# A fused decoder layer on one core: activations of the FFN output split beside the FFN's first products

## The chip, the core and the metric

The kernel runs on one core of a Trainium2 chip. The engines are TensorE (PE, with its weight loads as PEld), VectorE (DVE), ScalarE (ACT), GpSimd (POOL) and SyncE (SP), whose queue issues the transfers. The metric is the device time of one execution in microseconds (us).

## The reference, as far as it matters here

One decoder layer: a Mamba-2 mixer and an RG-LRU mixer side by side, then a SwiGLU feed-forward network (FFN) on 1024 positions of width 1024, hidden width 2816, all in float32. The change touches the FFN alone:

```python
hn = rmsnorm(h, norm2_w[l])
gate, up = jnp.split(hn @ w_ffn_in[l], 2, axis=-1)
h = h + (jax.nn.silu(gate) * up) @ w_ffn_out[l]
```

## The kernel before, in words

Data lie transposed: a tile has 128 features on the partitions and 1024 positions in two halves of 512. The hidden width is 22 such tiles (NFF), act_d[0] to act_d[21], kept in DRAM. A float32 product is done as three matmuls on operands that are split in two parts of reduced precision: hi is a cast (ScalarE, L98), lo is the value less hi (VectorE, L99), both in split. So one step of 128 by 128 by 512 is the three matmuls of product, L906 to L908.

Large products are done by a scheme of seven products in place of eight, on 2 by 2 blocks, with sums of operand blocks formed ahead. The activation operands of the seven are four blocks (b11, b21, b22 and b12, which is in the sums alone) and four sums t1 to t4; three of the blocks and the four sums are used.

**FFN, first products.** pair(n, ...) makes hidden tile n: gate and up weights, by the activations x2, which are split once and stay in the pool ar (20 of its 22 units) and in ar0. The seven products of a pair, in order, are a11·b11, s1·t1, s2·t2, a12·b21, s3·t3, s4·b22 and a22·t4, 12 matmuls each. The first, third, fifth and seventh go to one PSUM bank pu, which ScalarE copies after the first (L1250) and third (L1256), and which VectorE adds after the fifth (L1265) and reads after the seventh (L1272). In between the weights of the next pair are made: casts and subtractions (pair_a1, pair_s1, pair_s) and four sums on GpSimd (pair_sums, L1136 to L1139). finish_pair multiplies by the norm (L1204, L1206), takes the Silu (L1205), multiplies gate by up (L1207) and stores act_d[n]. After each product pump() puts a piece of other work into the program; ScalarE's instructions of a pair are pinned in the order in which they are written.

**t_store.** For the FFN output the sums t1 to t4 of the activations are made beforehand: eight calls of t_store in pairs 6 to 9 and 14 to 17, as work of pump(). Each loads two tiles of act_d, does four subtractions of half width (L301, L302, L304, L305) and stores two tiles t_d. In the order as built their instructions stand up to a pair earlier, so that pair 17 has none.

**FFN output.** seven(...) does 8 of the 22 hidden tiles by the scheme; it is called twice (NPART). A slot is half of one of the seven products: 24 matmuls. The second call's slots follow those of the first. Per product, load_xop loads four operand blocks of 128 by 512 (as two units xr of 512 KB) four slots ahead, x_part splits them two slots ahead, w_part splits weights and products runs. Its results are added to eight tiles res of the residual, which load_res loads. GpSimd forms the weight sums (w_sum, L960, L963). The slots before the first product are run beside the last pair (lead). The remaining six hidden tiles follow as plain products, then the last norm.

A pool's unit is a buffer of 128 by 1024 float32. Instructions of an engine run in the order in which the scheduler has put them; a buffer is used again when its last reader is done.

Of the kernel before, what the change touches and what calls it, by code (L numbers as in the profile page):

```python
# [8 lines left out]
F32 = mybir.dt.float32  # L9
F32R = mybir.dt.float32r  # L10
# [57 lines left out]
def hybrid_block(ctx, tc, xT, w_in, w_dt, w_os, w_ol, w_o, w_fi, w_fo, w_fl, lru_w, params, heads, out):  # L68
# [10 lines left out]
    def store(dst, src):  # L79
        nc.sync.dma_start(out=dst, in_=src)  # L80
# [200 lines left out]
    res_d = [dram.tile([P, T], F32, name=f"res_d{i}") for i in range(KD)]  # L281
    ty_d = [dram.tile([P, T], F32, name=f"ty_d{i}") for i in range(16)]
    tl_d = [dram.tile([P, T], F32, name=f"tl_d{i}") for i in range(8)]
    t_d = [dram.tile([P, T], F32, name=f"t_d{i}") for i in range(8 * NPART)]
    act_d = [dram.tile([P, T], F32, name=f"act_d{i}") for i in range(NFF)]

    def row(t_):
# [2 lines left out]
    def t_store(pool, src, dst, k, swap=False):  # L290


        u1, u2 = unit(pool, F32, "tu"), unit(pool, F32, "tu")
        for u, i in ((u1, k), (u2, k + 4)):
            if swap:
                for h in range(2):
                    load(u[:, h], src[i][:, hcol[1 - h]])
            else:
                load(row(u), src[i])
        yield  # L300
        V.tensor_tensor(u1[:, 0], u1[:, 1], u1[:, 0], op=ALU.subtract)  # L301
        V.tensor_tensor(u1[:, 1], u2[:, 1], u1[:, 1], op=ALU.subtract)  # L302
        yield
        V.tensor_tensor(u2[:, 1], u2[:, 1], u1[:, 0], op=ALU.subtract)  # L304
        V.tensor_tensor(u2[:, 0], u2[:, 0], u2[:, 1], op=ALU.subtract)  # L305
        store(dst[k], row(u1))
        store(dst[k + 4], row(u2))
        yield


# [609 lines left out]
        for f, a in events.pop(slot, ()):  # L920
            f(*a)

    def seven(c0_, act, tdf, w_of, out, pools=None, xpool=None, swap=False, done=None):


        pools = pools or {}
        wr, wop, xr_, xop, banks = {}, {}, {}, {}, {}

        def load_w(q, kh, g):

            if (q, kh) == (0, 0):
                t_ = wpool.tile([P, KD, P], F32, name="raw", tag="raw", bufs=2)
                t_ = t_.rearrange("p (a k) c -> p a k c", a=2)
            else:
                t_ = unit(pools.get((q, kh), ar), F32, "wr").rearrange("p a (k c) -> p a k c", c=P)
            for a in range(2):
                load(t_[:, a], w_of(q * 4 + 2 * g + a, kh))
            wr[q, kh, g] = t_

        def load_xop(n, kk):  # L940

            u = unit(xpool if xpool and n == N1 else ar, F32, "xr")
            src, o, h = {
                N2: (act, 4, 0), N5: (tdf, 0, 0), N3: (act, 4, 1), N1: (act, 0, 0),
                N6: (tdf, 4, 1), N7: (tdf, 0, 1), N4: (tdf, 4, 0),
            }[n]
            if swap and src is act:
                h = 1 - h
            for a in range(2):
                load(u[:, a], src[o + 2 * kk + a][:, hcol[h]])  # L950
            xr_[n, kk] = u

        def x_part(n, kk):
            hi, lo = (unit(xpool if xpool and n == N1 else ar, name=x) for x in ("xph", "xpl"))
            split(row(hi), row(lo), row(xr_.pop((n, kk))))
            xop.setdefault(n, []).extend((hi[:, a], lo[:, a]) for a in range(2))

        def w_sum(n, g):
            w = lambda q, kh: wr[q, kh, g]
            sub = lambda o, a, b: G.tensor_tensor(o, a, b, op=ALU.subtract)  # L960
            if n == 1:
                wr["s1", g] = unit(pools.get("s1", ar), F32, "ws").rearrange("p a (k c) -> p a k c", c=P)
                G.tensor_tensor(wr["s1", g], w(1, 0), w(1, 1), op=ALU.add)  # L963
            elif n == 2:
                sub(w(1, 0), w(0, 0), w(1, 0))
                sub(w(0, 0), wr["s1", g], w(0, 0))
            else:
                sub(w(0, 1), w(0, 1), w(0, 0))

        def w_part(n, g):  # L970
            key = {N2: (0, 1), N5: ("s1",), N3: (0, 1), N1: (0, 0), N6: (0, 0), N7: (1, 0), N4: (1, 1)}[n]
            hi, lo = (wpool.tile([P, 2, 4, P], F32R, name=x, tag=x) for x in ("whi", "wlo"))
            split(hi, lo, wr[(*key, g)])
            wop[n, g] = hi, lo

        def products(n, g):
            first, last = n in (N1, N2, N5), n in (N2, N3, N4)
            q, h = {N2: (0, 0), N5: (1, 1), N3: (0, 1), N1: (0, 0), N6: (0, 1), N7: (1, 1), N4: (1, 0)}[n]
            hi, lo = wop.pop((n, g))
            for a in range(2):  # L980
                p = 2 * g + a
                b = "x" if n == N2 else "v" if n in (N5, N3) else "u", p
                if first:
                    banks[b] = bank()
                product(banks[b], (hi[:, a], lo[:, a]), xop[n], first, last)
                d = q * 4 + p
                r, new = out(d, 1 - h if swap else h)
                if new and n in (N1, N5, N3, N4):
                    S.copy(r, banks[b])
                else:  # L990
                    V.tensor_tensor(r, r, banks[b], op=ALU.add)  # L991
                if done:
                    done(n, d)

        for g in range(2):
            at(c0_ - 4 + g, load_w, 0, 0, g)
            at(c0_ - 3 + g, load_w, 0, 1, g)
            at(c0_ - 2 + g, load_w, 1, 0, g)
            at(c0_ - 2 + g, load_w, 1, 1, g)
            for n in range(7):  # L1000
                at(c0_ + 2 * n - 4 + g, load_xop, n, g)
                at(c0_ + 2 * n - 2 + g, x_part, n, g)
                at(c0_ + 2 * n + g - 1, w_part, n, g)
                at(c0_ + 2 * n + g, products, n, g)
            for n in range(1, 4):
                at(c0_ + n + g, w_sum, n, g)
        rank = {f: r for r, f in enumerate((load_w, load_xop, w_part, x_part, w_sum, products))}
        for s in events:
            events[s].sort(key=lambda e: rank.get(e[0], 0 if e[0] not in later else 9))
# [274 lines left out]
    for i in range(NPART):  # L1284
        seven(
            i * CYC,
            act_d[8 * i : 8 * i + 8],
            t_d[8 * i : 8 * i + 8],
            lambda d, kh, i=i: w_fo[d, :, i * 8 + kh * 4 : i * 8 + kh * 4 + 4],
            lambda d, h: (res[d][:, h, :], False),  # L1290
            pools={"s1": wq, **({(1, 0): ar0} if i == 0 else {k: ar0 for k in ((0, 1), (1, 0), (1, 1))})},
        )
    for d in range(KD):
# [2 lines left out]


    todo = []

    def pump():  # L1300

# [11 lines left out]

    first_pair()
    for j in range(1, NFF):
        k = j - 6
        if 0 <= k < 8 * NPART and k % 8 < 4:
            todo.append(t_store(ar, act_d, t_d, k))
        if j == NFF - 1:
            todo.append(lead())  # L1320
        pair(j, None if j == NFF - 1 else j + 1, pump)
# [167 lines left out]
```

## Time and profile before

| | |
|---|---|
| median of 3 runs | 2103.59 us (2103.03 to 2105.32) |
| the profiled execution's own time | 2101.82 us |
| its span, first to last instruction | 2100.1 us |
| mean granted TensorE clock | 0.983 of full |
| TensorE busy | 2036.4 us, 97% |
| VectorE busy | 1395.7 us, 66% |
| ScalarE busy | 934.6 us, 45% |
| GpSimd busy | 538.0 us, 26% |

Times within the span are counted from its start. The pairs of the FFN's first products run from about 1440 to 1855, the two calls of seven from 1855 to 2020, the plain products and the last norm until 2100. Each engine has its own in-order queue; "idle before" names what ended an engine's wait. A busy share is a mean over stages, so the stage's own rows have to be read.

### The profile page before, as it was taken

What the parts mean: (1) busy time and instruction counts of PE and PEld (TensorE: products, weight loads), DVE (VectorE), ACT (ScalarE), POOL (GpSimd) and SP (SyncE); (2) the same over time, 40 slices, a digit from 0 to 9 for tenths busy, and PEclk for the clock granted to TensorE, in tenths of its full rate; (3) what the DMA queues carried; (4) which work ended last, traced back from release to release, by engine and by line L of the source; (5) the groups of instructions that cost most, each with busy time, mean ns of one, the idle gap of its engine ahead of it and who ended that gap; (6) DMA issues with size and microseconds to landing.
All of it is one profiled execution on the core that took longest, in us unless ns stands there. A gap on an engine that the chain in (4) does not pass through costs nothing. (4 is left out here: it accounts for less than half of the span.)

```text
span 2100.1 us, 24937 instructions
## 1 busy us (share of the span) xinstructions
PE 2036.4 (97%) x9506; PEld 1648.4 (78%) x9506; DVE 1395.7 (66%) x1618; ACT 934.6 (45%) x1291; POOL 538.0 (26%) x430
## 2 busy tenths in 40 slices
PE   8999999999999999999989999998999999989998
PEld 5677887887887888888868877776888888868888
DVE  8655567568667548666577868786466466578745
ACT  5334445445445436666643333453333333334334
POOL 5103333234333410000044042332322332242100
PEclk8999999999999999999989999999999999999999
DMA  4222223323223248244464613542254154276112
GB/s 141 86 64 87 89 76 118 100 67 121 93 76 115 89 160 316 95 157 157 154 205 160 231 55 118 165 154 82 74 181 157 66 179 171 86 281 209 61 59 88
DMA packets 121767, 269.85 MB, mean 128 GB/s; under 512 B 13616, under 2 KB 33072, under 8 KB 121648
## 3 DMA queue, kind: packets, MB, share of 16 engines
q1 hardware_dynamic: 121360, 267.22, 37.9%
q8 instruction: 74, 1.21, 0.2%
q10 hardware_dynamic: 288, 1.05, 0.1%
q14 instruction: 45, 0.37, 0.1%
HBM read 205.04 MB, written 63.18 MB: 128 GB/s over the span
## 5 line engine op out<-in xcount | busy, mean ns | idle before, releaser
L174 PE MATMUL pj<-hnh,whi 128*128 128x512 f32 x1152 | 461.3, 400 | 0.0
L176 PE MATMUL pj<-hnl,whi 128*128 128x512 f32 x1152 | 453.2, 393 | 0.0
L175 PE MATMUL pj<-hnh,wlo 128*128 128x512 f32 x1152 | 452.2, 393 | 0.0
L99 DVE TENSOR_TENSOR wlo<-raw,whi 128x1024 fp32r<-128x1024 f32 (+1 forms) x138 | 188.4, 1366 | 186.5 <-ACT whi L98 186.3
L176 PEld LDWEIGHTS pj<-hnl,whi 128*128 128x128 f32 x1152 | 216.8, 188 | 47.6 <-issue 0.5
L174 PEld LDWEIGHTS pj<-hnh,whi 128*128 128x128 f32 x1152 | 217.0, 188 | 45.7 <-issue 2.4
L175 PEld LDWEIGHTS pj<-hnh,wlo 128*128 128x128 f32 x1152 | 217.2, 189 | 44.8 <-issue 1.4
L906 PE MATMUL pbk<-xph,whi 128*128 128x512 f32 x560 | 222.5, 398 | 10.4 <-ACT xph L98 10.3
L908 PE MATMUL pbk<-xpl,whi 128*128 128x512 f32 x560 | 222.1, 398 | 10.1 <-DVE xpl L99 10.1
L907 PE MATMUL pbk<-xph,wlo 128*128 128x512 f32 x560 | 221.9, 396 | 3.2 <-DVE wlo L99 3.2
L98 ACT CAST whi<-raw 128x1024 fp32r<-128x1024 f32 (+1 forms) x138 | 142.5, 1033 | 79.8 <-PE pbk L908 29.4
L963 POOL TENSOR_TENSOR ws<-wr 128x1024 f32<-128x1024 f32 x10 | 29.2, 2920 | 454.1 <-DMA gate_d<-gl 297.0
L908 PEld LDWEIGHTS pbk<-xpl,whi 128*128 128x128 f32 x560 | 107.1, 191 | 36.3 <-DVE xpl L99 14.4
L906 PEld LDWEIGHTS pbk<-xph,whi 128*128 128x128 f32 x560 | 107.2, 191 | 35.3 <-ACT xph L98 13.2
L645 ACT ACTIVATE E<-csb,cs 128x128 f32<-128x128 f32 x256 | 82.8, 391 | 107.6 <-PE yb L686 100.4
L907 PEld LDWEIGHTS pbk<-xph,wlo 128*128 128x128 f32 x560 | 107.2, 191 | 28.1 <-DVE wlo L99 5.9
L99 DVE TENSOR_TENSOR xpl<-xr,xph 128x1024 fp32r<-128x1024 f32 x70 | 108.3, 1555 | 15.4 <-ACT xph L98 12.8
L906 PE MATMUL pbk<-xth,wsh 128*128 128x512 f32 x264 | 107.1, 406 | 4.8 <-DVE c L1228 4.6
L98 ACT CAST xph<-xr 128x1024 fp32r<-128x1024 f32 x70 | 72.9, 1050 | 81.4 <-DVE xpl L99 35.3
L907 PE MATMUL pbk<-xth,wsl 128*128 128x512 f32 x264 | 106.0, 401 | 0.0
L908 PE MATMUL pbk<-xtl,wsh 128*128 128x512 f32 x264 | 106.0, 401 | 0.0
L98 ACT CAST wsh<-raw 128x1024 fp32r<-128x1024 f32 x44 | 46.1, 1050 | 117.2 <-POOL raw L1139 92.4
(303 smaller groups left out, 4110.1 us busy)
## 6 DMA issues: line engine op xcount, KB each, us to landing
raw<-in_w_in SPq DMA_DIRECT2D x74, 512.0 KB, 3.5
raw<-in_w_fi SPq DMA_DIRECT2D x44, 512.0 KB, 3.7
csb<-cs_d SPq DMA_DIRECT2D x64, 256.0 KB, 3.6
act_d<-c SPq DMA_DIRECT2D x22, 512.0 KB, 3.9
yn_d<-xs SPq DMA_DIRECT2D x16, 512.0 KB, 3.4
tu<-yn_d SPq DMA_DIRECT2D x16, 512.0 KB, 6.2
ty_d<-tu SPq DMA_DIRECT2D x16, 512.0 KB, 4.2
xr<-ty_d SPq DMA_DIRECT2D x32, 256.0 KB, 3.4
```

The source lines that it names most:

```text
L98: ins = S.copy(hi, src)
L99: V.tensor_tensor(lo, src, hi.bitcast(F32), op=ALU.subtract)
L174: PE.matmul(ps, wh, xh, start=i == 0, stop=False)
L175: PE.matmul(ps, wl, xh, start=False, stop=False)
L176: PE.matmul(ps, wh, xl, start=False, stop=i == n - 1)
L645: S.activation(E[:, j, :], csb[:, j, :], AF.Relu, bias=cs[:, c, h0 + j : h0 + j + 1], scale=-1.0)
L906: PE.matmul(ps, wh, xh, start=first and k == 0, stop=False, skip_group_check=True)
L907: PE.matmul(ps, wl, xh, start=False, stop=False, skip_group_check=True)
L908: PE.matmul(ps, wh, xl, start=False, stop=last and k == n - 1, skip_group_check=True)
L963: G.tensor_tensor(wr["s1", g], w(1, 0), w(1, 1), op=ALU.add)
```

## The change

t_store of the FFN output and its tiles t_d go. In their place x_split, in every second pair from 6 to 20, loads two tiles of act_d, splits them as they are (the blocks b21, b22 and b11), forms the four sums, splits these too, and stores hi and lo of each of the seven operands side by side in a tile xs_d of DRAM: 14 stores of 256 KB each. hi and lo come from the pool br, which has six units and holds c0 and c1 of the pairs. In the FFN output load_xop loads a finished operand, hi and lo in one unit xp, three slots ahead in place of four, and x_part is not called. Uses in the earlier layers of the kernel keep x_part and t_store. Lines from L284 on are moved down: L1250 is now L1293, L1253 is L1296, L1256 is L1299, L1261 is L1304, L1265 is L1308, L1268 is L1311, L1272 is L1315, L1204 to L1207 are L1247 to L1250, L1136 to L1139 are L1179 to L1182.

```diff
-    t_d = [dram.tile([P, T], F32, name=f"t_d{i}") for i in range(8 * NPART)]
+    xs_d = [
+        [[dram.tile([P, 2, H], F32, name=f"xs_d{i}{n}{b}") for b in range(4)] for n in range(7)] for i in range(NPART)
+    ]
...
+    NX = ("b11", "b21", "t1", "b22", "t2", "t3", "t4")
+
+    def x_split(upool, pool, src, dst, k):
+        u1, u2 = unit(upool, F32, "tu"), unit(upool, F32, "tu")
+        load(row(u1), src[k])
+        load(row(u2), src[k + 4])
+        yield
+
+        def put(u, names):
+            hi, lo = unit(pool, name="xsh"), unit(pool, name="xsl")
+            split(row(hi), row(lo), row(u))
+            for a, n in enumerate(names):
+                if n:
+                    d = dst[NX.index(n)][k % 4]
+                    store(d[:, 0], hi[:, a].bitcast(F32))
+                    store(d[:, 1], lo[:, a].bitcast(F32))
+
+        put(u2, ("b21", "b22"))
+        yield
+        put(u1, ("b11", None))
+        yield
+        V.tensor_tensor(u1[:, 0], u1[:, 1], u1[:, 0], op=ALU.subtract)
+        V.tensor_tensor(u1[:, 1], u2[:, 1], u1[:, 1], op=ALU.subtract)
+        yield
+        V.tensor_tensor(u2[:, 1], u2[:, 1], u1[:, 0], op=ALU.subtract)
+        V.tensor_tensor(u2[:, 0], u2[:, 0], u2[:, 1], op=ALU.subtract)
+        yield
+        put(u1, ("t1", "t3"))
+        yield
+        put(u2, ("t4", "t2"))
         yield
...
         def load_xop(n, kk):
+            if pre:
+                for a in range(2):
+                    u = unit(xpool if xpool and n == N1 else ar, F32, "xp")
+                    load(row(u), pre[n][2 * kk + a].rearrange("p a b -> p (a b)"))
+                    xop.setdefault(n, []).append((u[:, 0].bitcast(F32R), u[:, 1].bitcast(F32R)))
+                return
...
-                at(c0_ + 2 * n - 4 + g, load_xop, n, g)
-                at(c0_ + 2 * n - 2 + g, x_part, n, g)
+                at(c0_ + 2 * n - (3 if pre else 4) + g, load_xop, n, g)
+                if not pre:
+                    at(c0_ + 2 * n - 2 + g, x_part, n, g)
...
     for i in range(NPART):
         seven(
             i * CYC,
-            act_d[8 * i : 8 * i + 8],
-            t_d[8 * i : 8 * i + 8],
+            None,
+            None,
...
+            pre=xs_d[i],
...
+    XSPLIT = (6, 8, 10, 12, 14, 16, 18, 20)
...
     for j in range(1, NFF):
-        k = j - 6
-        if 0 <= k < 8 * NPART and k % 8 < 4:
-            todo.append(t_store(ar, act_d, t_d, k))
+        if j in XSPLIT:
+            i = XSPLIT.index(j)
+            todo.append(x_split(ar, br, act_d[8 * (i // 4) :], xs_d[i // 4], i % 4))
```

How the instructions stand, at three places.

VectorE in pair 16, which had a t_store and now has an x_split. tu are the loaded tiles, wlo, ws1l and wsl the low parts of weights, c the pair's results, xsl the low parts of operands. Before:

```order
L301 TENSOR_TENSOR tu<-tu 128x512
L99 TENSOR_TENSOR wlo<-raw,whi 128x1024
L99 TENSOR_TENSOR ws1l<-ws_13384,ws1h 128x512
L1261 TENSOR_TENSOR c_13310<-c_13310,pbk 128x512
L302 TENSOR_TENSOR tu<-tu 128x512
L304 TENSOR_TENSOR tu<-tu 128x512
L305 TENSOR_TENSOR tu<-tu 128x512
L1265 TENSOR_TENSOR c_13311<-c_13311,pbk 128x512
L1206 TENSOR_TENSOR c_13311<-c_13311,rs_10486 128x512
L99 TENSOR_TENSOR wsl<-raw,wsh 128x1024
L1268 TENSOR_TENSOR c_13310<-c_13310,pbk 128x512
L1204 TENSOR_TENSOR c_13310<-c_13310,rs_10486 128x1024
```

Now, from the first split of the pair to its last instruction, in two pieces:

```order
L99 TENSOR_TENSOR xsl<-tu,xsh 128x1024 x2
L335 TENSOR_TENSOR tu<-tu 128x512
L99 TENSOR_TENSOR wlo<-raw,whi 128x1024
L1304 TENSOR_TENSOR c_13480<-c_13480,pbk 128x512
L336 TENSOR_TENSOR tu<-tu 128x512
L99 TENSOR_TENSOR ws1l<-ws_13562,ws1h 128x512
L338 TENSOR_TENSOR tu<-tu 128x512
L1308 TENSOR_TENSOR c_13481<-c_13481,pbk 128x512
L339 TENSOR_TENSOR tu<-tu 128x512
L99 TENSOR_TENSOR xsl<-tu,xsh 128x1024
L1249 TENSOR_TENSOR c_13481<-c_13481,rs_10526 128x512
```

```order
L1311 TENSOR_TENSOR c_13480<-c_13480,pbk 128x512
L99 TENSOR_TENSOR wsl<-raw,wsh 128x1024
L99 TENSOR_TENSOR xsl<-tu,xsh 128x1024
L1315 TENSOR_TENSOR c_13481<-pbk,rs_10526 128x512
L99 TENSOR_TENSOR wsl<-raw,wsh 128x1024
L1247 TENSOR_TENSOR c_13480<-c_13480,rs_10526 128x1024
L1250 TENSOR_TENSOR c_13480<-c_13480,c_13481 128x1024
```

Four full-width subtractions xsl have come in, and the subtractions of the sums stand between the weights' and the results' instructions.

ScalarE in the same pair, from the copy of the first product to that of the next pair. xsh are the high parts of operands, whi, ws1h and wsh those of weights. Before:

```order
L1250 COPY c_13310<-pbk 128x512
L1253 COPY c_13311<-pbk 128x512
L1256 COPY c_13310<-pbk 128x512
L98 CAST whi<-raw 128x1024
L98 CAST ws1h<-ws_13384 128x512
L98 CAST wsh<-raw 128x1024 x2
L1205 ACTIVATE c_13310<-c_13310 128x1024
L1250 COPY c_13446<-pbk 128x512
```

Now:

```order
L1293 COPY c_13480<-pbk 128x512
L1296 COPY c_13481<-pbk 128x512
L98 CAST xsh<-tu 128x1024 x2
L1299 COPY c_13480<-pbk 128x512
L98 CAST whi<-raw 128x1024
L98 CAST ws1h<-ws_13562 128x512
L98 CAST wsh<-raw 128x1024
L98 CAST xsh<-tu 128x1024 x2
L98 CAST wsh<-raw 128x1024
L1248 ACTIVATE c_13480<-c_13480 128x1024
L1293 COPY c_13644<-pbk 128x512
```

Two casts xsh stand ahead of the third product's copy, and two between the weights' casts; the Silu and the next pair's first copy follow as before.

SyncE's transfers ahead of the FFN output, in and behind the last pair (act_d_230, act_d_270 are hidden tile 20; act_d_231, act_d_271 tile 21; wr are weights, res the residual, xr and xp operands). Before, from the residual tiles on:

```order
L77 DMA res_14048<-res_d_165 128x1024
L77 DMA res_14050<-res_d_164 128x1024
L77 DMA res_14052<-res_d_163 128x1024
L77 DMA res_14054<-res_d_162 128x1024
L77 DMA xr<-act_d_212 128x512
L77 DMA xr<-act_d_213 128x512
L77 DMA wr<-in_w_fo 128x512 x4
L77 DMA xr<-act_d_214 128x512
L77 DMA xr<-act_d_215 128x512
L77 DMA wr<-in_w_fo 128x512 x4
L77 DMA xr<-act_d_216 128x512
L77 DMA xr<-act_d_217 128x512
```

The rows that followed were the store of act_d_231 and the other four res. Now, from the load of the second operand tile (xs_d_195) to the last of the second product (xs_d_201), in two pieces:

```order
L77 DMA xp<-xs_d_195 128x1024
L77 DMA wr<-in_w_fo 128x512 x4
L77 DMA xp<-xs_d_196 128x1024
L77 DMA xp<-xs_d_197 128x1024
L77 DMA res_14307<-res_d_165 128x1024
L77 DMA res_14309<-res_d_164 128x1024
L77 DMA res_14311<-res_d_163 128x1024
L77 DMA res_14313<-res_d_162 128x1024
L77 DMA wr<-in_w_fo 128x512 x4
L77 DMA xp<-xs_d_198 128x1024
L77 DMA xp<-xs_d_199 128x1024
```

```order
L80 DMA act_d_271<-c_14224 128x1024
L77 DMA res_14373<-res_d_169 128x1024
L77 DMA res_14375<-res_d_168 128x1024
L77 DMA res_14377<-res_d_167 128x1024
L77 DMA res_14379<-res_d_166 128x1024
L77 DMA xp<-xs_d_200 128x1024
L77 DMA xp<-xs_d_201 128x1024
```

The first four res have moved behind operands and weights, and all eight stand ahead of the last two tiles of the second product.

## Rows read from the trace of the kernel before

**Rows 1.** The page, first part: busy us (share of span) and instructions, TensorE.

```profile
PE 2036.4 (97%) x9506; PEld 1648.4 (78%) x9506; DVE 1395.7 (66%) x1618; ACT 934.6 (45%) x1291; POOL 538.0 (26%) x430
```

**Rows 2.** Who waited, 1440 to 1856: engine, line, releaser, us, times, longest.

```profile
PEld pbk L906 <- DVE c L1265: 2.8, 8, 0.7
```

**Rows 3.** Timeline, ScalarE, pairs 16 to 18: start, us, engine, line, [idle before].

```profile
1741.63 0.59 ACT L1250 COPY c<-pbk 128x512 f32<-128x512 f32 x1 [1.07 <-PE pbk L908]
...
1759.02 1.06 ACT L1205 ACTIVATE c<-c 128x1024 f32<-128x1024 f32 x1 [2.44 <-DVE c L1204]
...
1761.17 0.59 ACT L1250 COPY c<-pbk 128x512 f32<-128x512 f32 x1 [1.08 <-PE pbk L908]
...
1763.89 0.59 ACT L1253 COPY c<-pbk 128x512 f32<-128x512 f32 x1 [2.13 <-DMA raw<-in_w_fi]
...
1780.58 0.59 ACT L1250 COPY c<-pbk 128x512 f32<-128x512 f32 x1 [1.53 <-PE pbk L908]
```

**Rows 4.** Timeline, TensorE, the FFN output: first matmul, one wait, last matmul.

```profile
1855.29 0.39 PE L906 MATMUL pbk<-xph,whi 128*128 128x512 f32 x1
...
1857.73 0.50 PE L908 MATMUL pbk<-xpl,whi 128*128 128x512 f32 x1 [1.59 <-DVE xpl L99]
...
2019.59 0.39 PE L908 MATMUL pbk<-xpl,whi 128*128 128x512 f32 x1
```

**Rows 5.** Who TensorE waited for, 1855 to 2000.

```profile
PE pbk L908 <- DVE xpl L99: 4.1, 3, 2.1
PE pbk L906 <- ACT xph L98: 2.1, 1, 2.1
PE pbk L907 <- DVE wlo L99: 1.0, 2, 0.8
```

**Rows 6.** Stretches: length, PE, PEld, DVE, ACT, POOL busy, clock, DMA, GB/s.

```profile
1847.00:1875.00 28.00, 22.51 (x92) 16.79 (x90) 20.86 (x17) 10.99 (x11) 17.49 (x7) 0.93 0.95 344
1855.00:1860.00 5.00, 3.41 (x15) 2.48 (x15) 4.90 (x5) 1.99 (x2) 0.55 (x2) 1.00 0.93 333
1872.00:1876.00 4.00, 1.70 (x4) 0.98 (x4) 4.00 (x3) 2.56 (x3) 4.00 (x2) 0.50 1.05 392
1876.00:1880.00 4.00, 3.62 (x9) 2.33 (x9) 4.00 (x2) 0.00 (x0) 4.00 (x2) 0.50 0.45 166
```

**Rows 7.** Timeline, VectorE, the FFN output's early splits of activations.

```profile
1872.06 10.02 DVE L99 TENSOR_TENSOR xpl<-xr,xph 128x1024 fp32r<-128x1024 f32 x3
```

**Rows 8.** Timeline, VectorE, full-width instructions back to back.

```profile
1837.85 1.22 DVE L1207 TENSOR_TENSOR c<-c,c 128x1024 f32<-128x1024 f32 x1
1838.99 1.22 DVE L99 TENSOR_TENSOR wlo<-raw,whi 128x1024 fp32r<-128x1024 f32 x1
```

**Rows 9.** Timeline, VectorE, in pair 16, which has a t_store.

```profile
1750.46 0.68 DVE L1261 TENSOR_TENSOR c<-c,pbk 128x512 f32<-128x512 f32 x1
1751.06 1.19 DVE L302 TENSOR_TENSOR tu<-tu 128x512 f32<-128x512 f32 x1
1752.28 1.67 DVE L304 TENSOR_TENSOR tu<-tu 128x512 f32<-128x512 f32 x1
1753.98 0.69 DVE L305 TENSOR_TENSOR tu<-tu 128x512 f32<-128x512 f32 x1
1754.59 0.68 DVE L1265 TENSOR_TENSOR c<-c,pbk 128x512 f32<-128x512 f32 x1
```

**Rows 10.** Timeline, GpSimd's weight sums in pair 16.

```profile
1745.35 1.29 POOL L1136 TENSOR_TENSOR ws<-raw 128x512 f32<-128x512 f32 x1 [11.48 <-DMA raw<-in_w_fi]
...
1750.09 1.61 POOL L1138 TENSOR_TENSOR raw<-ws,raw 128x512 f32<-128x512 f32 x1 [2.07 <-DVE wlo L99]
...
1751.78 1.62 POOL L1139 TENSOR_TENSOR raw<-raw 128x512 f32<-128x512 f32 x1
```

**Rows 11.** Timeline, SyncE's DMA issues, pair 21: start, us of issuing.

```profile
1839.46 5.98 SPq L77 DMA_DIRECT2D res<-res_d  x4
...
1847.55 0.80 SPq L77 DMA_DIRECT2D xr<-act_d  x2
```

More of the change, by code (lines that the diff above doesn't have):

```diff
@@ L307, in t_store @@
         store(dst[k + 4], row(u2))
+        yield
[24 more added lines that the diff above has]
+        put(u1, ("t1", "t3"))
+        yield
+        put(u2, ("t4", "t2"))
         yield
@@ L921, in run, with seven @@
             f(*a)
-    def seven(c0_, act, tdf, w_of, out, pools=None, xpool=None, swap=False, done=None):
+    def seven(c0_, act, tdf, w_of, out, pools=None, xpool=None, swap=False, done=None, pre=None):
         pools = pools or {}
```

## The prediction

> **What bounds the kernel now.** Read the page's first part first: TensorE is busy 97% of the span [rows 1]. A change can then gain only where TensorE stands, and loses wherever it makes TensorE stand. So the next view is who TensorE waits for in the two stages that the change touches.
>
> In the FFN's first products (pairs 1 to 21) it waits for almost nothing. One row [rows 2] is the one to learn from: eight times a weight load waited for VectorE's L1265, 2.8 us together and 0.7 at most. Eight is the number of t_store calls here. Already the four half-width subtractions of a t_store bring VectorE to the edge of a pair. L1265 adds the fifth product's bank and so frees it for the seventh product.
>
> ScalarE's rows [rows 3] give the beat. L1250 copies the first product's bank, 1761.17 and 1780.58 in the next pair: 19.41 us without a t_store. The pair before, with one, took 1761.17 - 1741.63 = 19.54. From L1250 to L1253, 2.72 us, is one product of 12 matmuls, 0.227 us each.
>
> In the FFN output the first and the last matmul stand 164.3 us apart [rows 4]; 672 matmuls of 0.227 are 152.3, so 12.2 us are lost (with the last matmul's own 0.2). The waits that the trace names make 4.1 + 2.1 + 1.0 = 7.2 of them [rows 5], all behind splits on ScalarE and VectorE; the other 5.0 are small gaps and the clock, which stood at 0.50 of full, 1.2 GHz, from 1872 to 1880 [rows 6]. Behind the longest stretch is one row [rows 7]: three splits that take 1.14 us elsewhere [rows 8] needed 10.02, beside GpSimd's weight sums. These 12.2 us are all that the change can win back there.
>
> **What goes from the FFN output.** 28 splits of activations per engine, 1.14 us each on VectorE, leave this stage. The three slow ones with them, so I take the waits on operand splits as gone. That is the gain: at most 12.2 us, if nothing else comes late.
>
> **What comes into the pairs.** Eight x_splits in pairs 6, 8, ... 20, each wholly inside one pair. Each has the four half-width subtractions of a t_store, plus four full-width splits (one cast on ScalarE and one subtraction on VectorE each), plus 14 stores of 256 KB for two of 512.
>
> I time such a pair by the order of its VectorE instructions, with time 0 at its L1250 copy (L1293 now). The second copy ends 2.72 + 0.59 = 3.31 later. The first cast of an x_split stands behind it and takes 1.05 as the other casts, so VectorE's first split starts at 4.36. From there to the multiplication by the norm (L1247, formerly L1204), the order has 18 instructions: eight of full width, 1.14 us from start to start [rows 8], and ten of half width, 0.60 [rows 9]. That is 9.12 + 6.00 = 15.12 us without a gap.
>
> Then waits on GpSimd. The half-width subtraction that takes 0.60 took 1.22 and 1.70 from start to start beside GpSimd's second pair of sums, while additions that read a PSUM bank, at 1750.46, went by in 0.60 [rows 9]. Each finished just after a sum did [rows 10]: a VectorE instruction with both inputs in SBUF stands while a sum runs. This costs 0.62 + 1.10 = 1.72 us, as it does now. The first two sums, 1.29 us each, begin 3.72 after the copy, one behind the other [rows 3, 10], where VectorE idles now. There the first two new splits will stand. The trace has no such meeting in a pair; the bounds are 0 and 2 x 1.29 = 2.58. I take 0.65 for what is left of the first sum at 4.36 and 1.29 for the second, 1.94, since the splits of the output stage waited for whole sums [rows 7].
>
> L1247 thus ends at 4.36 + 15.12 + 1.72 + 1.94 = 23.14. The Silu behind it on ScalarE takes 1.06 [rows 3] and ends at 24.20. ScalarE is in order: the next pair's L1293 copy stands behind this Silu, and ends at 24.79. The third product of the next pair adds into the bank that this copy reads, and would start at 19.41 + 2.72 = 22.13. So it is **2.66 us late**. (About 1.3 of that falls already before the seventh product: L1308, behind eight instructions of 6.42 us and the same waits, ends at 4.36 + 6.42 + 3.66 + 0.60 = 15.04, and six products end at 5 x 2.75 = 13.8.) The pair after has no x_split and VectorE catches up, so nothing adds up beyond this.
>
> Eight times 2.66 is 21.3 us; the eight t_stores' own 0.13 each, 1.0 in all, go: **+20.3 us**. With no waits for the first two sums it would be 8 x 0.72 - 1 = +4.8, with the full 2.58 it would be 8 x 3.30 - 1 = +25.4. The casts, 4.2 us of ScalarE per pair, cost nothing beyond this: the first two fill its 2.13 us of idling ahead of a copy [rows 3], the other two wait for VectorE. The transfers of such a pair (14 stores, two operand loads, two weight loads and one store of activations, 6.3 MB in 19.4 us or 325 GB/s) stay below the 344 seen over 28 us [rows 6]; if this cover went, the weights, GpSimd's sums and with them L1308 would come later still.
>
> **The transfers ahead of the FFN output.** The operands now come as two parts, 2 MB for each of the seven products where 1 MB came. They need units of the pool ar, which holds the operands of the last pair until its fifth product. Now the first load that needs one is issued at 1847.55, 7.74 us before the output's first matmul [rows 4, 11]. In the new order of the queue, a load of the second operand tile stands at that point, and the residual tiles that went out at 1839.46, while the units were still held [rows 11], have moved behind it. From there to the last tile of the second product (xs_d_201) I count seven operand tiles, eight residual tiles, four half-MB pieces of weights and one store, 20 pieces of 0.524 MB or 10.5 MB, where 14 loads of 0.262 stood before the corresponding tile. At 344 GB/s [rows 6] this takes 30.5 us and ends 22.8 after the output's first matmul. The second product needs that tile after 48 + 9 matmuls, 12.9 us. **9.9 us late.** The nearest other rate, 392 GB/s over 4 us [rows 6], makes it 6.2.
>
> The Trainium skill (DMA: Bandwidth & Descriptors, Where 436 GB/s comes from) gives about 358 GB/s as one core's share of HBM; by that it would be 8.7 late and my sum 1.2 us shorter. The 392 of the trace lies above this figure, so it is no hard limit here.
>
> After such a wait I expect the clock at 1.2 GHz again, as from 1872 on, and leave the 5.0 us of clock and small gaps as they are: 9.9 + 5.0 = 14.9 us lost in place of 12.2, **+2.7**. At 392 GB/s it is 6.2 + 5.0, or -1.0; with twice the clock loss of now (5.3 us of matmuls ran at half speed from 1872 to 1880 [rows 6], 2.7 lost) and as much again for transfers that start late, it is +8.
>
> **Sum.** The profiled execution took 2101.82 us, 1.77 below the median of the runs. 2101.8 + 20.3 + 2.7 = 2124.8 on that basis; as a median, 2126.6. Forecast **2127 us**. What a measurement can tell from no change is 0.2%, 4 us.
>
> **The rivals.**
> 1. The operands land in time. For it: the queue runs ahead and some units may free earlier. Against: 10.5 MB in 20 us would be 510 GB/s, which no stretch shows. Were it so, the output stage would lose some 3 us for 12.2: 2127 - 12 = 2115.
> 2. Faster, the other side: the pairs hide the splits. The point that decides is VectorE's margin: 22.13 - 0.59 - 1.06 - 15.12 - 4.36 = 1.0 us of waiting per pair. Against: 1.72 are waited already by the rows of now. With it hidden, -1 us in the pairs, and -9 in the output if its operands come in time too: 2103.6 - 10 = 2094.
> 3. No difference: pairs hide the splits (-1) and the output's transfers take back its gain (+2.7): 2105.
> 4. The clock falls in the pairs. A fall at the output cost 2.7 us above; with five falls among the sixteen waits it is 2127 + 13 = 2140. Against: from 1855 to 1860, with a wait of 1.59 us in it [rows 4], the clock stayed at 1.00 [rows 6], and my waits are no longer and over 5 us apart.
>
> **How the numbers follow.** The forecast's own case 0.57, its range 2107 to 2137 by the bounds above (+4.8 - 1.0 and +25.4 + 8, and 1.8 to the median). Rival 1, 0.18; rival 2, 0.08; rival 3, 0.08; rival 4, 0.09. The range 2103 to 2138 leaves out rival 2 and most of rival 4. Faster 0.09, the same 0.08, slower 0.83.
>
> **What would show it.** Right: TensorE rows that wait on VectorE's L1308 and on ScalarE's L1293, about eight of each and over 1 us; full-width xsl splits of over 2 us beside GpSimd's L1179 and L1180; pairs of 20.7 and 20.8 us where an x_split sits or has just sat; in the output's first 25 us one wait of several us that ends with a transfer of xs_d, and a clock of 0.50 behind it; no split waits there. Wrong: pairs of 19.4 us throughout, with L1247 ending before 21 us after its copy; or an output stage of less than 157 us.

## The result, and the profile after

The changed kernel takes 2115.69 us (median of 4 runs, 2114.18 to 2117.61), the kernel before, on the same chip, 2103.31 (2102.39 to 2105.32). The ratio is 1.0057, 95% interval 1.0045 to 1.007: slower by 12.4 us, where 23 were forecast. The profiled execution took 2115.78 us with a span of 2114.1, 14.0 more than before. The profiled execution before had been 1.5 below its own median, which is the difference between 14.0 and 12.4. All of the following sums are made on the spans.

The page's first part, to be held against [rows 1] (busy us, share of the span, instructions):

```profile
PE 2037.0 (96%) x9506; PEld 1645.6 (78%) x9506; DVE 1403.2 (66%) x1622; ACT 935.3 (44%) x1295; POOL 537.8 (25%) x430
```

TensorE does the same work and is busy for the same time; its share fell because it stands longer. So the first view is again whom it waits for, in the FFN's first products (engine, line, releaser: us in all, times, longest):

```profile
PE pbk L942 <- ACT c L1293: 8.9, 8, 1.1
PE pbk L942 <- DVE c L1308: 6.0, 8, 0.8
PE pbk L942 <- DVE c L1271: 4.5, 1, 4.5
```

The third row is the first pair's and was there before the change. The first two are new, eight times each, once for every x_split. In TensorE's timeline of pairs 16 and 17 they are these:

```profile
1767.48 0.50 PE L942 MATMUL pbk<-xth,wsh 128*128 128x512 f32 x1 [0.73 <-DVE c L1308]
...
1777.12 0.50 PE L942 MATMUL pbk<-xth,wsh 128*128 128x512 f32 x1 [1.11 <-ACT c L1293]
```

ScalarE's timeline shows how they fall into the beat (start, us, engine, line, idle before), for the answer to [rows 3]:

```profile
1752.97 0.59 ACT L1293 COPY c<-pbk 128x512 f32<-128x512 f32 x1 [1.58 <-PE pbk L944]
...
1775.53 1.06 ACT L1248 ACTIVATE c<-c 128x1024 f32<-128x1024 f32 x1 [5.43 <-DVE c L1247]
1776.50 0.57 ACT L1293 COPY c<-pbk 128x512 f32<-128x512 f32 x1
...
1794.15 0.59 ACT L1293 COPY c<-pbk 128x512 f32<-128x512 f32 x1 [1.57 <-PE pbk L944]
```

Pair 16 takes 23.53 us and pair 17 takes 17.65. The short pair does not mean a fast TensorE: its first copy came late, because ScalarE stood 5.43 us for VectorE's L1247 and then did the Silu. Two pairs take 41.18 where 38.82 is the beat of before, 2.36 us for each x_split.

VectorE in the same pair, answering to [rows 9]:

```profile
1757.21 3.47 DVE L99 TENSOR_TENSOR xsl<-tu,xsh 128x1024 fp32r<-128x1024 f32 x2 [4.05 <-ACT xsh L98]
...
1762.46 0.68 DVE L1304 TENSOR_TENSOR c<-c,pbk 128x512 f32<-128x512 f32 x1
1763.05 1.47 DVE L336 TENSOR_TENSOR tu<-tu 128x512 f32<-128x512 f32 x1
1764.45 1.78 DVE L99 TENSOR_TENSOR ws1l<-ws,ws1h 128x512 fp32r<-128x512 f32 x1
...
1766.75 0.68 DVE L1308 TENSOR_TENSOR c<-c,pbk 128x512 f32<-128x512 f32 x1
...
1774.29 1.21 DVE L1247 TENSOR_TENSOR c<-c,rs 128x1024 f32<-128x1024 f32 x1
```

And GpSimd's sums, answering to [rows 10]:

```profile
1756.01 1.29 POOL L1179 TENSOR_TENSOR ws<-raw 128x512 f32<-128x512 f32 x1 [11.03 <-DMA raw<-in_w_fi]
1757.38 2.22 POOL L1180 TENSOR_TENSOR raw<-raw 128x512 f32<-128x512 f32 x1
1762.68 1.30 POOL L1181 TENSOR_TENSOR raw<-ws,raw 128x512 f32<-128x512 f32 x1 [3.09 <-DVE wlo L99]
1764.06 1.62 POOL L1182 TENSOR_TENSOR raw<-raw 128x512 f32<-128x512 f32 x1
```

The two xsl splits have the first two sums beside them, of L1179 only its last 0.1 us; L336 and ws1l have the other two. L1304, which reads a PSUM bank and runs while L1181 starts, takes its plain 0.68. The sum loses time too: L1180 took 2.22 us beside the splits and 1.30 in pair 17, which has none.

In the FFN output TensorE's timeline answers to [rows 4] and its named waits to [rows 5]:

```profile
1873.66 0.39 PE L942 MATMUL pbk<-xp,whi 128*128 128x512 f32 x1
...
1885.70 0.47 PE L942 MATMUL pbk<-xp,whi 128*128 128x512 f32 x1 [0.46 <-DMA xp<-xs_d]
...
1894.49 0.50 PE L942 MATMUL pbk<-xp,whi 128*128 128x512 f32 x1 [2.31 <-DMA xp<-xs_d]
...
1895.77 0.80 PE L942 MATMUL pbk<-xp,whi 128*128 128x512 f32 x1 [0.22 <-DMA xp<-xs_d]
...
2033.45 0.39 PE L944 MATMUL pbk<-xp,whi 128*128 128x512 f32 x1
```

```profile
PE pbk L942 <- DMA xp<-xs_d: 3.0, 3, 2.3
PE pbk L943 <- DVE wlo L99: 1.1, 2, 0.7
```

The stage takes 159.8 us where it took 164.3. The waits on splits of activations are gone; three short ones on transfers have come. The stretches around the longest (length, busy PE, PEld, DVE, ACT, POOL, clock, DMA share, GB/s) answer to [rows 6]:

```profile
1895.00:1897.00 2.00, 1.78 (x5) 1.06 (x5) 0.00 (x0) 0.00 (x0) 2.00 (x1) 0.55 1.02 412
...
1875.00:1903.00 28.00, 23.90 (x92) 17.61 (x91) 10.72 (x12) 4.85 (x5) 17.44 (x7) 0.94 1.03 407
```

Behind the wait of 2.31 the clock stood near 1.2 GHz (0.55 of full in the first of the two stretches) for some 3 us, and the transfers ran at 407 GB/s over 28 us.

The account of the 14.0 us: the pairs, from the second pair's first copy (1449.92, before 1449.16) to the output's first matmul, took 423.7 us for 406.1, **+17.6**; the output **-4.5**; what lies ahead of the pairs +0.8 and behind the output +0.1.

### The profile page after: what moved, and what is told of

It reads as the page before. It is cut to its first block, busy times and chain, and to the rows that moved or that the text cites. A ratio compares the mean times of both kernels' runs of the same rounds, so it can differ in the third digit from the quotient of the medians.

```text
span 2114.1 us, 25171 instructions
## 1 busy us (share of the span) xinstructions
PE 2037.0 (96%) x9506; PEld 1645.6 (78%) x9506; DVE 1403.2 (66%) x1622; ACT 935.3 (44%) x1295; POOL 537.8 (25%) x430
## 3 DMA queue, kind: packets, MB, share of 16 engines
q8 instruction: 74, 1.21, 0.2%
## 5 line engine op out<-in xcount | busy, mean ns | idle before, releaser
L942 PE MATMUL pbk<-xph,whi 128*128 128x512 f32 x336 | 134.0, 399 | 8.8 <-ACT xph L98 8.8
L944 PE MATMUL pbk<-xpl,whi 128*128 128x512 f32 x336 | 134.3, 400 | 5.3 <-DVE xpl L99 5.3
L943 PE MATMUL pbk<-xph,wlo 128*128 128x512 f32 x336 | 133.6, 398 | 2.9 <-DVE wlo L99 2.9
L942 PE MATMUL pbk<-xth,wsh 128*128 128x512 f32 x264 | 107.2, 406 | 19.5 <-ACT c L1293 8.9
L1033 DVE TENSOR_TENSOR res<-res,pbk 128x512 f32<-128x512 f32 x96 | 65.1, 683 | 73.5 <-PE pbk L944 73.3
L943 PE MATMUL pbk<-xth,wsl 128*128 128x512 f32 x264 | 105.1, 398 | 0.0
L1179 POOL TENSOR_TENSOR ws<-raw 128x512 f32<-128x512 f32 x22 | 29.0, 1319 | 252.7 <-DMA raw<-in_w_fi 241.7
L942 PE MATMUL pbk<-xp,whi 128*128 128x512 f32 x224 | 88.3, 394 | 3.0 <-DMA xp<-xs_d 3.0
L943 PE MATMUL pbk<-xp,wlo 128*128 128x512 f32 x224 | 88.0, 393 | 1.1 <-DVE wlo L99 1.1
L944 PE MATMUL pbk<-xp,whi 128*128 128x512 f32 x224 | 87.5, 392 | 0.0
```

The lines of the kernel that those rows point to most:

```text
L942: PE.matmul(ps, wh, xh, start=first and k == 0, stop=False, skip_group_check=True)
L943: PE.matmul(ps, wl, xh, start=False, stop=False, skip_group_check=True)
L944: PE.matmul(ps, wh, xl, start=False, stop=last and k == n - 1, skip_group_check=True)
L1179: G.tensor_tensor(blk(s1), u_[:, 0:4, :], u_[:, 4:8, :], op=ALU.add)
```

## The experiments

Theory: in a pair with an x_split VectorE's in-order chain is too long, counted in its own instructions and in the time it stands beside GpSimd's sums. Rivals: the new transfers, or ScalarE's new casts. For the output: the order of the transfer queue. In each run "pairs" is the time from the second pair's first copy to the output's first matmul (changed kernel 423.7), "output" that from its first to its last matmul (159.8). The runs fell on several chips, on which the kernel before took 2101.5 to 2103.3 us; so whole times are compared by their ratio to it, and stages by the traces.

**No low parts.** In put of x_split:

```diff
-            hi, lo = unit(pool, name="xsh"), unit(pool, name="xsl")
-            split(row(hi), row(lo), row(u))
+            hi = unit(pool, name="xsh")
+            S.copy(row(hi), row(u))
...
-                    store(d[:, 1], lo[:, a].bitcast(F32))
+                    store(d[:, 1], hi[:, a].bitcast(F32))
```

> Edit: in x_split the low part is not subtracted; the high part is stored in its place, so the casts, the stores and the loads stay and eight times four full-width VectorE subtractions go (the FFN output is computed with a wrong low part). Theory: an x_split's pair is late because VectorE's chain is too long, and without 4 x 1.14 = 4.56 us of it L1247 ends about 4.6 earlier, well before the 22.13 that the third product needs. All pairs then take 19.4 to 19.6 us in place of 23.5 and 17.7 in turn, and the time falls by 8 x 2.36 = 18.9, to 2096 to 2099 us. Rival one, transfers: the 14 stores of an x_split delay weights and so the pair. Then pairs stay at 23.5 and 17.7 and the time at 2113 to 2117. Rival two, ScalarE's four casts: the same, no gain.

Measured: 2091.88 us, ratio to before 0.9952 (0.9933 to 0.997). The first copies of pairs 16 to 18:

```profile
1739.97 0.59 ACT L1293 COPY c<-pbk 128x512 f32<-128x512 f32 x1 [1.53 <-PE pbk L944]
...
1759.43 0.59 ACT L1293 COPY c<-pbk 128x512 f32<-128x512 f32 x1 [1.52 <-PE pbk L944]
...
1778.80 0.59 ACT L1293 COPY c<-pbk 128x512 f32<-128x512 f32 x1 [1.53 <-PE pbk L944]
```

19.46 and 19.37: the pairs are at TensorE's beat, though the casts, the loads and all 14 stores are still there. Pairs 404.8, 19.0 less. The two rivals fall. (Without xsl the first two sums meet only L335, for 0.3 us, so this run also takes away most of the first meeting.) The time came out below the range by 4 us and more, because the output was shorter too, 154.7; what made it so this run doesn't settle.

**No weight sums.** In pair_sums:

```diff
-        s1 = sp1.tile([P, H], F32, name="ws1", tag="ws1")
-        wops[n]["raw1"] = s1
-        G.tensor_tensor(blk(s1), u_[:, 0:4, :], u_[:, 4:8, :], op=ALU.add)
...
+        wops[n]["raw1"] = u_[:, 0:4, :].rearrange("p k c -> p (k c)")
```

> Edit: GpSimd's four weight sums of a pair are left out, and the split of s1 takes half of the up weights in their place (the FFN's products are then computed from wrong weights). VectorE's instructions, ScalarE's and the transfers stay. Theory: of the 23.5 us of a pair 3.1 are VectorE standing while a GpSimd sum runs. Without the sums L1247 ends at about 4.36 + 15.12 = 19.5 after its copy, the next copy at 21.1, 1.0 before it is needed: pairs at 19.4 to 19.6, time 2096 to 2100 us. The rival, that the number of VectorE instructions alone is too large, whatever GpSimd does: pairs stay uneven, at 22.5 to 23.5 and 17.7, time 2108 to 2116.

Measured: 2082.30 us, ratio 0.9906 (0.9888 to 0.9924). VectorE in a pair with an x_split, and the first copies of that pair and the next two (lines are five lower here, L1288 is the copy):

```profile
1731.82 2.36 DVE L99 TENSOR_TENSOR xsl<-tu,xsh 128x1024 fp32r<-128x1024 f32 x2 [4.04 <-ACT xsh L98]
...
1736.56 0.68 DVE L336 TENSOR_TENSOR tu<-tu 128x512 f32<-128x512 f32 x1
1737.16 0.68 DVE L99 TENSOR_TENSOR ws1l<-raw,ws1h 128x512 fp32r<-128x512 f32 x1
```

```profile
1727.58 0.59 ACT L1288 COPY c<-pbk 128x512 f32<-128x512 f32 x1 [1.57 <-PE pbk L944]
...
1748.23 0.56 ACT L1288 COPY c<-pbk 128x512 f32<-128x512 f32 x1
...
1766.41 0.59 ACT L1288 COPY c<-pbk 128x512 f32<-128x512 f32 x1 [1.57 <-PE pbk L944]
```

The two splits take 2.36 for 3.47, L336 0.68 for 1.47, ws1l 0.68 for 1.78: this is the time that VectorE stood beside GpSimd, and nothing else in the chain was removed. Pairs 404.8 again. The pairs are still uneven, 20.65 and 18.18, and I had expected them even; yet they add up to 38.83, the beat of before, and TensorE has no wait left in this stage. A copy that is 1.2 us late costs nothing, since the third product needs it only 2.72 after the copy's normal time. So the four subtractions fit without the meetings, and the second meeting fits without the subtractions; both together are too long. The rest of the gain, 13.6 us, lies ahead of the second pair, which begins at 1436.3: the first pair's waits go too, nearly all of them on VectorE and the 4.5 us of L1271 above among them. The named ones make 8.8 of the 13.6; the rest isn't traced, and in the other runs this point alone varies by 6 us. The expectation had forgotten that pair.

**Spread.** Each x_split over 13 pieces of other work in place of 7, by doubled yields:

```diff
+        yield
         put(u2, ("b21", "b22"))
         yield
+        yield
...
-    XSPLIT = (6, 8, 10, 12, 14, 16, 18, 20)
+    XSPLIT = (5, 13)
...
-            todo.append(x_split(ar, br, act_d[8 * (i // 4) :], xs_d[i // 4], i % 4))
+            todo.append(iter((None,) * 3))
+            for k in range(4):
+                todo.append(x_split(ar, br, act_d[8 * i :], xs_d[i], k))
```

> Edit: the same x_splits, each over 13 pieces of pump() in place of 7, so about two pairs for one; two chains of four, begun in the middle of pairs 5 and 13. Theory: the work of an x_split fits if no pair gets more than half of it. VectorE's chain in the worst pair is then about 12.8 us where it was 15.1, the lateness 0 to 0.4 a pair: time 2097 to 2102 us, below the kernel before by some 0.2%, since the FFN output keeps its gain. Rival: the sum over all pairs counts (each GpSimd meeting costs where it stands, now in every pair): 2108 to 2116.

Measured: 2097.42 us (10 runs), ratio 0.9976 (0.9967 to 0.9985): faster than before, as expected. Pairs 409.2, output 156.4. In two places TensorE still waits for the addition after the fifth product (L1314 here). One of them is the pair at 1645.7 to 1667.3, 21.55 us long, where the scheduler has put two xsl and three of the x_split's four half-width subtractions ahead of that addition. The two xsl began with GpSimd's first sum here and met both, so they took 4.48 us where 3.47 stood. VectorE's rows and TensorE's behind them:

```profile
1649.98 4.48 DVE L99 TENSOR_TENSOR xsl<-tu,xsh 128x1024 fp32r<-128x1024 f32 x2 [2.66 <-ACT xsh L98]
...
1660.66 0.68 DVE L1314 TENSOR_TENSOR c<-c,pbk 128x512 f32<-128x512 f32 x1
```

```profile
1661.40 0.50 PE L948 MATMUL pbk<-xth,wsh 128*128 128x512 f32 x1 [1.88 <-DVE c L1314]
```

**Residual tiles later.** The changed kernel with one line of the schedule changed:

```diff
-        at(-1 + d // 4, load_res, d)
-        events[-1 + d // 4].insert(0, events[-1 + d // 4].pop())
+        s = -1 + 3 * (d // 4)
+        at(s, load_res, d)
+        events[s].insert(0, events[s].pop())
```

> Edit: the second four residual tiles are loaded three slots later (slot 3 in place of 0 counted from their old place), so the last two operand tiles of the second product go out ahead of them. Theory: TensorE's wait of 2.31 + 0.22 us for these tiles is the queue's order. 2.1 MB less ahead of them is 5.2 us at the 400 GB/s of this stretch; the waits go, and with them 0.8 us at a lower clock: 2.5 to 3.5 us faster, 2112 to 2113.5. Rival: the stretch is bound by bytes, and a later tile is late by as much: 2115 to 2116, with a wait of 2 us on another transfer.

Measured: 2110.25 us, ratio 1.0035 (1.0022 to 1.0049). Output 154.5, pairs 423.6. TensorE's waits in the output:

```profile
PE pbk L942 <- DMA xp<-xs_d: 0.9, 1, 0.9
PE pbk L943 <- DVE wlo L99: 0.4, 1, 0.4
```

The wait of 2.31 is gone and no later transfer is late in its place, although the bytes are the same; the wait that is left stands on the second product's first tile, where 0.46 stood. The clock stayed at full speed through this stretch, and the stage gave 5.3 us, more than the 2.5 to 3.5 expected: the small gaps behind the waits went with them.

**The split of b11 at half width**, on the changed kernel:

```diff
-            split(row(hi), row(lo), row(u))
+            c = slice(0, 2 if names[1] else 1)
+            split(hi[:, c], lo[:, c], u[:, c])
```

> Edit on the changed kernel: of the split of u1 as it is only the half that is stored (b11) is done: one of the eight full-width VectorE instructions of the chain becomes half width. Theory, chain length: each x_split is 1.14 - 0.60 = 0.54 us less late, two pairs take 40.6 in place of 41.18, time 8 x 0.54 = 4.3 us below the changed kernel. Rival, meetings with GpSimd: the instruction only moves the following ones into a sum's time, and nothing or less than 1.5 us is won.

Measured: 2111.07 us, ratio 1.0048 (1.0033 to 1.0062), which the runs can't tell from the changed kernel's 1.0057. In the trace two pairs take 40.8 where they took 41.18: 0.4 won of 0.54. That is 3.3 us over the eight, nearer to the theory's 4.3 than to the rival's 1.5. TensorE's waits in the pairs (L1309 here is L1308, L943 is L942) and two VectorE rows:

```profile
PE pbk L943 <- DVE c L1309: 11.8, 8, 1.6
```

```profile
1759.92 1.21 DVE L99 TENSOR_TENSOR xsl<-tu,xsh 128x1024 fp32r<-128x1024 f32 x1
1761.06 0.67 DVE L1309 TENSOR_TENSOR c<-c,pbk 128x512 f32<-128x512 f32 x1
```

The wait for the copy is gone from the list, but that for the addition doubled, from 6.0 to 11.8: the scheduler has moved one more xsl ahead of it. The chain is shorter, and less of it was won than left, because what counts is what stands ahead of the first instruction that TensorE needs.

**The Silu later.** finish_pair of a pair is written after the next pair's third copy:

```diff
         order(S.copy(c0[:, 1, :], pu))
+        while ended_pair:
+            finish_pair(*ended_pair.pop())
         prep(pair_a1)
...
-        finish_pair(n, c0, c1)
+        ended_pair.append((n, c0, c1))
+        if nxt is None:
+            finish_pair(*ended_pair.pop())
```

> Edit on the changed kernel: finish_pair of a pair is written after the next pair's third copy, so that ScalarE's copy of the next pair's first bank no longer stands behind the Silu. VectorE's number of instructions stays. Theory: of the 2.36 us that an x_split costs about 1.1 are the next pair's third product waiting for that copy and 1.2 the seventh product waiting for L1308. The first part goes: 8 x 1.1 = 8.9 us below the changed kernel, and no row of TensorE waiting for the copy after the first product. In this kernel's order one xsl has moved into the pair before, which can take some of the other part too: 8 to 16 us. Rival, VectorE as such: with the same work in the pair the wait moves to another row (L1308, or c's bank) and the gain is under 4 us.

Measured: 2117.58 us, ratio 1.0078 (1.0064 to 1.0093). The theory's numbers fell, the rival's came. TensorE in the pairs (L1312 here is L1308), and VectorE in a pair with an x_split:

```profile
PE pbk L942 <- DVE c L1312: 15.8, 8, 2.6
```

```profile
1756.36 1.23 DVE L99 TENSOR_TENSOR xsl<-tu,xsh 128x1024 fp32r<-128x1024 f32 x1 [2.66 <-ACT xsh L98]
1759.17 2.04 DVE L1250 TENSOR_TENSOR c<-c,c 128x1024 f32<-128x1024 f32 x1 [1.58 <-ACT c L1248]
...
1767.40 0.67 DVE L1312 TENSOR_TENSOR c<-c,pbk 128x512 f32<-128x512 f32 x1
```

No row waits for the copy any more, as the theory had it. But L1250 needs the Silu and now stands at the head of the pair's VectorE work: VectorE idles 1.58 us for it, runs it beside GpSimd's L1180 in 2.04, and L1312 ends 15.96 us after the pair's first copy (1752.11), where L1308 ended at 14.46. The loss has moved from one row to the other: pairs 424.2 for 423.7. The output took 161.7 for 159.8, with 5.0 us of waits on transfers for 3.0; why it is longer, this run doesn't settle.

**Together.** Spread, residual tiles later and half b11:

> Edit: the spread x_splits and the later residual tiles together, and the split of b11 at half width (its other half is not stored). Theory: the two gains lie in different stages and add where both had a loss left. The spread run lost 4.5 us in the pairs against an even 19.4 each and 4.1 in the FFN output against 152.3; half of a full-width split less, 0.54 us, takes 1 to 2 of the first, the queue's order 1.5 to 2 of the second: 3 to 4 us below the spread run, 2093 to 2095 us on a chip where before takes 2102.6. Rival: the spread already gave the output its order, since its transfers were issued earlier; then 2096 to 2098.

Measured: 2091.97 us, ratio 0.9963 (0.995 to 0.9977), 1 us below the expected range on a chip where before took 1 us less than assumed. Pairs 409.0, the two long pairs at 21.55 and 21.53 with L1315 (L1308) as their row; half b11 won nothing there. Output 152.1, and the whole stage in one stretch:

```profile
1857.00:2011.00 154.00, 154.00 (x681) 127.53 (x680) 83.73 (x95) 34.32 (x37) 40.90 (x16) 1.00 0.67 250
```

TensorE is busy throughout, at 2.4 GHz: nothing is left to win in this stage. With the later Silu on top:

> Edit: spread, residual tiles later, half b11 and the later Silu together. Theory: what is left of waits in the pairs is 1 to 2 us and in the FFN output 2: 2090 to 2094 us on a chip where before takes 2102.6. Rival: the later Silu holds c tiles of the pool br longer, and xsh waits for a unit: no faster than without it, 2094 to 2097.

Measured: 2099.47 us (11 runs), ratio 0.9989 (0.998 to 0.9998), slower than without it; pairs 413.7, with 6.6 us of TensorE's waits for the same addition. Two rows stand ahead of it, VectorE's and ScalarE's in pairs 6 to 21 (L1257 is L1250, L1255 the Silu):

```profile
DVE c L1257 <- ACT c L1255: 31.2, 14, 7.5
```

```profile
ACT xsh L98 <- DMA xs_d<-xsh: 5.6, 2, 2.9
```

VectorE stands for the Silu in nearly every pair, as with the later Silu alone; and two casts waited until an earlier xsh was stored, which is the rival's reason. Which of the two weighs more isn't separated.

**Spread evenly.** Pieces set so that no pair has more than 3.54 us of an x_split's VectorE work ahead of the addition, by the order of the instructions:

```diff
-            todo.append(iter((None,) * 3))
+            todo.append(iter((None,) * 1))
```

with the yields of x_split at 1, 2, 3, 2, 3, 2 and 1 behind its seven pieces.

> Edit on the run of spread, residual tiles later and half b11: the pieces lie a little apart (an x_split over 14 pieces, the first of them sooner, more room around the sums), so that by the order of VectorE's instructions no pair has more than 3.54 us of an x_split ahead of the addition after the fifth product, where 4.14 stood in four pairs. Theory, that addition decides: of the 4 us that the two pairs of 21.5 still lose, 3 to 4 go, pairs at 19.4 to 19.7 apart from the last: 2087 to 2090 us where before takes 2101.5 to 2102.6. Rival: those two pairs are uneven for another reason (a weight or GpSimd's sum that comes late after the last piece of one x_split and the load of the next), then 2091 to 2093.

Measured: 2091.93 us, ratio 0.9948 (0.9935 to 0.9962). Pairs 404.7, as without low parts, and TensorE has no named wait from the second pair to the last: the theory of the addition holds, and all that the x_splits cost is hidden. But against the run "Together" without the later Silu (0.9963) the intervals overlap, so a gain isn't shown. The profiled execution lost the 4.3 us of the pairs again: the second pair began 1.6 later, behind a wait of 1.4 on an earlier xtl that the other run did not have, and the output took 154.8 for 152.1, with this row:

```profile
PE pbk L951 <- DVE wlo L99: 1.5, 1, 1.5
```

The 1.6 tells nothing of the edit: over the profiled executions of all runs but the one without weight sums, whose edits leave the work ahead of the second pair alone, its first copy lies between 1445.4 (half b11) and 1451.8 (residual tiles later). Whether the output lost its part because TensorE now arrives there earlier, these runs don't tell. Both versions beat the kernel before, by 0.4 and 0.5%.

## Why the prediction was right in its direction and 11 us too high

- **What bounds the kernel, and the sign.** Right. The pairs had no room for the x_splits, and the rows named ahead came: L1308 and L1293, eight times each. They were 0.7 to 0.8 and 1.1 us long; over 1 us was right for one of the two. Of the other signs, the pairs of 20.7 and 20.8 did not come: the copies stand 23.53 and 17.65 apart, because the copy itself is late, with a sum of 41.18 for 41.5. Nor did xsl of over 2 us: two took 3.47.
- **The pairs, +20.3.** Measured +17.6. An x_split costs 2.36 where 2.66 stood; the two runs that take away the subtractions or the sums show that both parts of the sum were needed. L1247 ended 22.53 after the copy (1774.29 + 1.21 - 1752.97) where 23.14 was forecast, so the chain of 18 instructions was right within 0.6. The term that was mis-sized is the meeting with the first two sums: 1.94 taken, 3.47 - 2.36 = 1.1 measured. The sums began 3.04 us after the copy where 3.72 was taken (1756.01 - 1752.97), so L1179 was nearly over when the first xsl started. The second meeting was forecast at 1.72 and measured at 0.79 + 1.10 = 1.9. What is left comes to little: the first matmul behind each of the two waits is 0.11 longer (0.50 for 0.39 in the rows above). Of the gain in place of the t_stores, 1.0 was right. Another 0.4 came from a pair that took 19.94 before, where the others with a t_store took 19.53; it has no match after.
- **Transfers and casts of the pairs cost nothing.** Right, as the run without low parts shows. The row read for it, 2.13 us of idling ahead of L1253, is that of the second copy; the first two casts stand ahead of the third, where ScalarE idled up to 2.2 before.
- **The transfers of the output, +2.7.** Wrong in sign: the output gave 4.5 back. The queue's order was read rightly: the second operand tile went out 7.74 us before the first matmul, and the last tile of the second product was there 22.1 after it, 22.8 forecast. That the two agree so well is partly luck, for between these two moments the transfers ran at 391 GB/s in place of 344, and moved 11.7 MB in place of the 10.5 that I counted; transfers issued before or behind the counted ones had a share. The step that failed is "The second product needs that tile after 48 + 9 matmuls". In the trace 24 matmuls stand between TensorE's wait for the first tile of the second product (1885.70) and that for the third (1894.49), where the text of the code has 6: the product takes its first two operand tiles through all four outputs before it touches the third. So the third is needed after 72 matmuls and xs_d_201 after 75, four us later than I had. TensorE had also lost some 2 us by then in two waits of 0.46 and in small gaps, so it reached the third tile 18.5 after its first matmul, and waited 2.31 us, then 0.22: 3.0 us with the earlier one, in place of 9.9. (At 392 GB/s the prediction's sum gives 6.1 and not 6.2.) I had shown the queue's order from the program and taken TensorE's from the text of the code.
- **Clock and small gaps, 5.0.** Mis-sized: 159.8 - 152.3 = 7.5 us are lost, 4.1 in named waits, 3.4 in the rest. Where the waits went, the rest went with them. It was a price of the waits and not one of the stage.
- **The rivals.** The first, operands in time, gives 2115 by its arithmetic, and that is the time measured; but that is luck in part, since its cause holds by half: three waits on operands are there, and the pairs lost less than it took over from the forecast. The others didn't come. The clock stayed at full speed in the pairs. The second needed pairs that hide the splits: the changed kernel doesn't, but the even spread does, with 404.7 us, and its time then is 2092, where that rival said 2094.

## What to carry to other kernels

Work put beside a stage that TensorE fills costs nothing as long as the first instruction that TensorE needs is not late; so count what stands ahead of that instruction on its in-order engine, with the time lost beside other engines, for the fullest pair and not for the mean. The same work spread over two pairs, in pieces, turned 0.6% slower into 0.2% faster, and 0.4 to 0.5% with the residual tiles put behind the operands that are used first; halving the half-used split won nothing there. When a transfer's due time is part of a sum, read it from the order of the instructions that use it.

## What the runs showed of the hardware

- A VectorE instruction that reads two tiles in SBUF takes longer beside a GpSimd sum: 1.47 and 1.78 us with the sums, 0.68 and 0.68 without. The sum can lose too, 2.22 for 1.30. A VectorE instruction that reads a PSUM bank loses nothing (0.68 for L1304, and for L1261 in [rows 9] beside the sum at 1750.09 of [rows 10]). The Trainium skill (SBUF — State Buffer, Who interferes with whom) has this rule; the runs agree, and show that it took 3.0 us of a pair of 23.5.
- The transfers ran at 407 GB/s for 28 us, and at 408 to 412 in stretches of 5 us of the run with all three edits. In the prediction I had taken 344, from 28 us of the kernel before, and had this core's 392 over 4 us only as the nearest other rate.
- How long TensorE had stood did not by itself decide whether the clock fell. It went to 0.50 of full, 1.2 GHz, behind the 4.55 us of the first pair (before and after), behind the 2.31 of the output, and behind 1.78 us in the output of the spread run. It stayed at 1.00 behind 1.88 us in the pairs of that same run, and behind 2.59 in a pair of the run with the later Silu; of the six waits of 2.00 to 2.02 there it fell behind one, that of the pair shown, which took 23.22 us where most took 21.65. What decides is open here.
